# Strided attention: scores in two column halves, one turn of the weights, outputs over 64 rows

## The chip, the cores and the metric

The kernel runs on one core of a Trainium2 chip. The metric is the device time of one execution in microseconds. Three runs of the kernel before took 131.04, 131.12 and 131.29 us (median 131.12). One profiled execution of it took 130.88 us; its trace spans 129.0 us, and the remaining 1.8 us lie outside the first and the last instruction.

## The reference

```python
attend_positions = np.arange(0, seq, stride)          # 1024 / 64 = 16 keys per head
k = K[:, :, attend_positions, :]; v = V[:, :, attend_positions, :]
scores = einsum('bhqd,bhkd->bhqk', q, k) / sqrt(dim)  # every query, 16 keys
weights = exp(scores - max); weights /= sum + 1e-10
result = einsum('bhqk,bhkd->bhqd', weights, v)
```

Q, K, V and the result are (8, 12, 1024, 64) in fp32: 96 heads of 1024 queries with 64 elements. Q (25.2 MB) is read whole, of K and V every 64th row, and the result (25.2 MB) is written whole.

## The kernel before, in words

The 96 heads are worked in 24 groups of four (`NG`, index `g`). A group of Q is 1 MB; it lands in one of 16 buffers (`big[:, g % 16]`, 8 KB on each of 128 partitions), and the group's result is later written into the same buffer and stored from there. So the load of group g + 16 waits until the store of group g has landed.

For one group the engines do this:

- ACT (`cast_a`) and POOL (`cast_p`) cast the two halves of Q to bf16 (`qb`).
- DVE turns it in 32x32 blocks of bf16 pairs (`turn`, L362) into `qt`: the partitions then hold head (4) and pair of the 64 elements (32), the two elements of a pair lie side by side, and the columns are the tokens.
- PE makes the scores (`score_products`, L561). The stationary operand `k_cur` holds two heads' 16 keys in 32 columns. Two passes `f` (one for each element of a pair) add up; within a pass four matmuls of 32 columns and 512 tokens go to the four quarters of the array's columns (`tile_position`). The moving operand's innermost step is one pair, 4 bytes, 32 times.
- DVE turns the scores back from PSUM so that tokens lie on partitions (`lay`, L389) and takes the maximum over 16 keys (`highest`, L396).
- POOL subtracts it (L403), ACT takes the exponent (L409), DVE adds up (`sums`, L414) and inverts (`inverse`, L421), POOL multiplies and casts to bf16 (`normalise`, L428).
- DVE turns the weights (`back`, L438) in two operations of 64 partitions each. They fill the two diagonal blocks of `w_t`, a 128x128 matrix for each of 8 token sets; the other two blocks were set to zero once, at the start (L291).
- PE multiplies `w_t` with the values (`output_products`, L573): for each half `h` four matmuls over all 128 rows, 256 columns each. `v_cur` holds the four heads' values, each masked to its own rows.
- ACT copies the outputs from PSUM into the buffer (`evict`, L455), twice for a group.

Nothing is scheduled by a tool: the order is written out by hand. In the steady state DVE runs a loop of 20 groups (`dve_stream`, four rounds in its body) with the order `lay(g)`, `turn(g+1)`, `highest(g)`, `sums(g-1)`, `back(g-2)`, `inverse(g-1)`. PE runs a loop of its own: `score_products(g+3)`, then `output_products(g, 0)` and `(g, 1)`. Engines wait for each other through counting semaphores (`gates`). ACT and POOL run straight programs whose order follows the loop over `n`.

All transfers are issued by SP on one queue, in the order: the loads of 16 groups with the rows of K and V among the first, two stores, then store g and load g + 14 in turn for g = 2 to 9, then stores of two groups at once, the last of them (groups 22 and 23) after everything else. A store (`send`, L251) writes from each partition runs of 16 tokens, 4 KB.

Of the kernel before, what the change touches and what calls it, by code (L numbers as in the profile page):

```python
# [11 lines left out]
BF16 = mybir.dt.bfloat16  # L12
I16 = mybir.dt.int16
I32 = mybir.dt.int32
# [160 lines left out]
def kernel(  # L175
# [8 lines left out]
    nc = tc.nc  # L184
# [22 lines left out]
    k_all = sb.tile([P, NG, 2, 2, 32], BF16, name="k_all")  # L207
    identity = sb.tile([P, P], BF16, name="identity")
    perm_v = sb.tile([P, 2, 2, 2, 2, NK], BF16, name="perm_v")
# [12 lines left out]
    k_cur = sb.tile([P, 2, 2, 2, 32], BF16, name="k_cur")  # L222
    s_sel = sb.tile([P, 4], FP32, name="s_sel")

    spare, later = big[:, NB - 1], big[:, NB - 2]
# [47 lines left out]
    def constants():  # L273
        op("POOL", lambda: nc.gpsimd.memset(identity, 0.0), writes=["identity"])
        op("POOL", lambda: nc.gpsimd.affine_select(
            out=identity, in_=identity, compare_op=ALU.not_equal, fill=1.0, base=0,
            pattern=[[-1, P]], channel_multiplier=1,
        ), reads=["identity"], writes=["identity"])
        for c in range(2):
            for b in range(2):  # L280
                op("POOL", lambda c=c, b=b: nc.gpsimd.tensor_copy(
                    out=perm_v[:, c, b],
                    in_=_ap_with(
                        identity, [identity.ap[0], [0, 2], [32, 2], [1, NK]], 64 * c + 16 * b
                    ),
                ), reads=["identity"], writes=[f"perm{c}{b}"])
# [5 lines left out]
        op("DVE", lambda: nc.vector.tensor_reduce(  # L292
            out=s_sel,
            in_=identity.rearrange("p (b e u k) -> p u e b k", b=2, e=2, u=2),
            op=ALU.max, axis=mybir.AxisListType.XY,
        ), reads=["identity"], writes=["s_sel"])

# [7 lines left out]

    def keys(c, s, e):
        fn = nc.vector.tensor_copy if e == "DVE" else nc.scalar.copy
        src, b, u = 32 * (2 * c + s // 2), s % 2, s // 2
        op(e, lambda: fn(  # L309
            k_all[32 * s : 32 * s + 32, c::2, :, b, NK * u : NK * u + NK],  # L310
            k_r[src : src + 32].rearrange("p n (a k f) -> p a n f k", a=2, f=2)[:, b],
        ), reads=["k_r", "k_zero"], writes=[f"k{c}{s}"])

    def value_sums(n):
        for c in range(2):
            r = nc.tensor.matmul(  # L316
                o_ps[n][:, c, 0 : NC * D // 2],
                lhsT=perm_v[:, n].rearrange("p b e u k -> p (b e u k)"),
                rhs=v_bf[:, 6 * c : 6 * c + 6], start=True, stop=True,
            )  # L320
        return r

    def value_rows():
        op("POOL", lambda: nc.gpsimd.tensor_copy(out=v_bf, in_=v_raw), reads=["v_raw"],  # L324
           writes=["v_bf"], gate="stV")
        for n in range(2):
            op("PE", None, reads=["v_bf"] + [f"perm{n}{b}" for b in range(2)],
               writes=[f"o{n}"], gates=[("stV", 1)])

    def value_copy(n):  # L330
# [37 lines left out]
    def place_k(g):  # L368
        n = 1 if g < 2 else 2
        op("POOL", lambda: nc.gpsimd.tensor_copy(  # L370
            out=k_cur[:, g % 2 : g % 2 + n].rearrange("p g f b x -> p (g f b x)").bitcast(I32),
            in_=k_all[:, g : g + n].rearrange("p g f b x -> p (g f b x)").bitcast(I32),
        ), reads=["k_zero"] + [f"k{i % 2}{s}" for i in range(g, g + n) for s in range(4)],
           writes=[f"k_cur{i % 2}" for i in range(g, g + n)], gate=None if g == 1 else "stK")

# [50 lines left out]

    def normalise(g):
        op("POOL", lambda: nc.gpsimd.tensor_tensor(  # L428
            out=_ap_with(w_n[g % 2], [w_n[g % 2].ap[0], [64, 8], [1, 2], [32, 2], [2, NK]]),
            in0=ex[g % 2][:, :, 0:NK].rearrange("p (t x u) k -> p t x u k", x=2, u=2),  # L430
            in1=rec[g % 2].rearrange("p (t x u) -> p t x u", x=2, u=2).unsqueeze(4).to_broadcast([P, 8, 2, 2, NK]),
            op=ALU.mult,
        ), reads=[f"ex{g % 2}", f"rec{g % 2}"], writes=[f"w_n{g % 2}"], gate="wn")

    def back(g):
        for b in range(2):
            rows = slice(64 * b, 64 * b + 64)
            r = nc.vector.transpose(  # L438
                w_t[g % 2][rows, :, rows].bitcast(I32),
                w_n[g % 2][rows].rearrange("p n k -> p (n k)").bitcast(I32),  # L440
            )
        return r

    def weights_back(g, **how):
        op("DVE", lambda: back(g), reads=[f"w_n{g % 2}"], writes=[f"w_t{g % 2}"], gate="wt",
# [4 lines left out]
           gates=[("ev", 2 * g + h + 1)] + [("wt", g + 1)] * (h == 0) + [("stV", g // 2 + 2)] * (h == g % 2 == 0))  # L450

    def evict(g, h):
        o = o_ps[h].rearrange("p c (t x d) -> p x (c t) d", t=2, d=D)
        to = big[:, g % NB].rearrange("p (x t d) -> p x t d", x=4, t=8)[:, :, 4 * h : 4 * h + 4]
        op("ACT", lambda: nc.scalar.copy(to, o), reads=[f"o{h}"], writes=[f"b{g % NB}{'ab'[h]}"],  # L455
           gate=None if g == NG - 1 or (g, h) == (NG - 3, 1) else "ev")

# [95 lines left out]
    def pe_stream(sems, gates):  # L553
        pe = nc.tensor

        def score_products(g):
            for f in range(2):
                for e in range(2):
                    for b in range(2):
                        c = 2 * b + e  # L560
                        r = pe.matmul(  # L561
                            sc_ps[g % 2][32 * c : 32 * c + 32], lhsT=k_cur[:, g % 2, f, b],
                            rhs=_ap_with(
                                qt[g % 2], [qt[g % 2].ap[0], [D, 8], [16 * D, 2], [2, 32]],
                                extra_offset=8 * D * e + f,
                            ),
                            start=f == 0, stop=f == 1, tile_position=(0, 32 * c),
                        )
            r.then_inc(gates["sc"], 1)

        def output_products(g, h):
            for t in range(4):
                r = pe.matmul(  # L573
                    o_ps[h][:, t // 2, 256 * (t % 2) : 256 * (t % 2) + 256],
                    lhsT=w_t[g % 2][:, 4 * h + t],
                    rhs=v_cur[:, g % 2].rearrange("p x d -> p (x d)"),
                    start=True, stop=True,
                )
            r.then_inc(sems["PE"], 1)

        pe.wait_ge(gates["stV"], 1)
        for n in range(2):
            value_sums(n).then_inc(sems["PE"], 1)
        for g in range(AHEAD):
            pe.wait_ge(gates["turned"], g + 1)
            if g % 2 == 0:
                pe.wait_ge(gates["stK"], g // 2 + 1)
            score_products(g)
        with pe.Fori(0, NG // TURN):
            for j in range(TURN):  # L590
                pe.wait_ge(gates["turned"], j + AHEAD + 1)
                if j:
                    pe.wait_ge(gates["stK"], (j + AHEAD) // 2 + 1)
                score_products(j + AHEAD)
                for h in range(2):
                    pe.wait_ge(gates["ev"], 2 * j + h + 1)
                    if h == 0:
                        pe.wait_ge(gates["wt"], j + 1)
                        if j == 0:
                            pe.wait_ge(gates["stV"], 2)  # L600
                    output_products(j, h)
            for name, n in (("turned", TURN), ("wt", TURN), ("ev", 2 * TURN), ("stK", 1), ("stV", 1)):
                pe.sem_inc(gates[name], -n)
# [64 lines left out]
```

## Time and profile before

| what | before |
|---|---|
| median of three runs | 131.12 us |
| the profiled execution, its span | 130.88 us, 129.0 us |
| busy: DVE, ACT, POOL, PE | 107.5, 90.3, 84.2, 66.9 us |
| bytes moved, mean rate over the span | 51.15 MB, 396 GB/s |
| DMA queue of SP: share of 16 engines' time | 94.7% |
| one 64x256 turn of the weights (48 of them) | 435 ns |
| two score passes of one group on PE | 1.04 us |
| eight output matmuls of one group on PE | 1.87 us |

An engine's busy time counts overlapping instructions once. The chain of waits follows the work that ended last back from the end. The table of stages gives for any stretch the busy time of each engine, the granted clock of PE, the share of the 16 DMA engines' time that packets took, and the rate.

### The profile page before, as it was taken

To read this page: it belongs to the slowest core of one execution; us is meant where nothing else is said; L and a number is where in the kernel's file an instruction comes from. 1 tells how busy PE (TensorE), PEld (TensorE's weight loads), DVE (VectorE), ACT (ScalarE), POOL (GpSimd) and SP (SyncE) were. 2 spreads that over 40 slices of the span, in tenths; PEclk is the share of its full clock that TensorE was granted. 3 is DMA by queue.
4 is the path that set the end of the run, shared out by engine and by line. 5 is a ranking of instruction groups with operands and counts; after the bars stand their busy time and mean duration, and the time that the engine had idled before them with its cause. 6 is when DMAs were issued, how large, how long until landed. Compare 5 with 4: busy or idle time off the path is not lost.

```text
span 129.0 us, 1514 instructions
## 1 busy us (share of the span) xinstructions
PE 66.9 (52%) x412; PEld 26.4 (20%) x412; DVE 107.5 (83%) x185; ACT 90.3 (70%) x106; POOL 84.2 (65%) x110
## 2 busy tenths in 40 slices
PE   0000620338766654667865478666486668498000
PEld 0000100003332122312332123321133213234000
DVE  4739699499999999999999999999999999982000
ACT  3034877747788998798879888789877876778400
POOL 4016650949777987779877797777977777643000
PEclk9999999999999999555558655557855555959955
DMA  3999999999999899998998998998999996396993
GB/s 71 341 385 470 427 396 467 437 396 457 416 427 447 361 429 424 434 485 366 437 477 366 455 470 361 460 480 361 432 442 411 416 432 269 163 472 259 452 442 163
DMA packets 6803, 51.15 MB, mean 396 GB/s; under 512 B 3760, under 2 KB 3760, under 8 KB 3760
## 3 DMA queue, kind: packets, MB, share of 16 engines
q1 hardware_dynamic: 6800, 51.12, 94.7%
q14 instruction: 3, 0.02, 0.1%
HBM read 25.95 MB, written 25.17 MB: 396 GB/s over the span
## 4 chain that ended last, share of the span: by engine, by line
DVE 70%; DMA 6%; PE 4%; issue 4%; POOL 3%; ACT 2%; SPq 2%; DVEq 1%; ACTq 1%; POOLq 0%
DVE qt L362 20%; DVE s_t L389 11%; DVE w_t L438 11%; DVE top L396 11%; DVE total L414 11%; DMA big<-in_V_dram 6%; DVE rec L421 6%; PE o L573 2%; DVE v_all L340 2%; PE sc L561 1%; SPq L34 1%; POOL w_n L428 1%; POOL s_t L403 1%; ACT big L455 1%; ACT qb L353 1%
## 5 line engine op out<-in xcount | busy, mean ns | idle before, releaser
L455 ACT COPY big<-o 128x1024 f32<-128x1024 f32 x48 | 46.3, 1016 | 14.1 <-PE o L573 14.1
L573 PE MATMUL o<-v_cur,w_t 128*128 128x256 bf16 x192 | 39.1, 371 | 22.8 <-DVE w_t L438 20.8
L428 POOL TENSOR_TENSOR w_n<-ex,rec 128x512 bf16<-128x512 f32 x24 | 25.5, 1061 | 15.9 <-DVE rec L421 15.9
L561 PE MATMUL sc<-qt,k_cur 128*32 128x512 bf16 x216 | 26.6, 584 | 17.1 <-DVE qt L362 10.6
L573 PEld LDWEIGHTS o<-v_cur,w_t 128*128 128x128 bf16 x192 | 22.3, 125 | 49.6 <-issue 39.8
L403 POOL TENSOR_TENSOR s_t<-s_t,top 128x512 f32<-128x512 f32 x24 | 25.4, 1058 | 7.1 <-DVE top L396 7.1
L362 DVE STREAM_TRANSPOSE qt<-qb 128x1024 int32<-128x1024 int32 x24 | 28.8, 1200 | 0.0
L353 ACT CAST qb<-big 128x1024 bf16<-128x1024 f32 x24 | 25.2, 1055 | 0.0
L358 POOL CAST qb<-big 128x1024 bf16<-128x1024 f32 x24 | 25.0, 1044 | 0.1
L438 DVE STREAM_TRANSPOSE w_t<-w_n 64x256 int32<-64x256 int32 x48 | 20.9, 435 | 1.9 <-POOL w_n L428 1.6
L409 ACT ACTIVATE ex<-s_t 128x512 f32<-128x512 f32 x24 | 15.3, 638 | 6.8 <-POOL s_t L403 6.8
L389 DVE STREAM_TRANSPOSE s_t<-sc 128x512 f32<-128x512 f32 x24 | 15.8, 660 | 1.6 <-PE sc L561 1.6
L414 DVE TENSOR_REDUCE total<-ex 128x32 f32<-128x544 f32 x24 | 16.9, 706 | 0.0
L396 DVE TENSOR_REDUCE top<-s_t 128x32 f32<-128x512 f32 x24 | 15.5, 647 | 0.1
L561 PEld LDWEIGHTS sc<-qt,k_cur 128*32 128x32 bf16 x216 | 3.7, 104 | 30.2 <-DVE qt L362 22.8
L421 DVE RECIPROCAL rec<-total 128x32 f32<-128x32 f32 x24 | 8.5, 353 | 0.7
L316 PE MATMUL o<-big,perm_v 128*128 128x384 bf16 x4 | 1.5, 521 | 12.7 <-POOL big L324 12.7
L378 POOL COPY v_cur<-v_all 128x256 int32<-128x256 int32 (+1 forms) x13 | 5.0, 384 | 1.1 <-PE o L573 1.1
L370 POOL COPY k_cur<-k_all 128x128 int32<-128x128 int32 (+1 forms) x13 | 3.7, 281 | 2.1 <-ACT k_all L309 1.8
L299 ACT CAST big<-big 128x384 bf16<-128x384 f32 x1 | 0.5, 512 | 5.4 <-DMA big<-in_K_dram 5.4
L300 POOL CAST big<-big 128x384 bf16<-128x384 f32 x1 | 0.5, 507 | 5.3 <-DMA big<-in_K_dram 5.3
L309 DVE COPY k_all<-big 32x384 bf16<-32x384 bf16 x6 | 3.5, 588 | 0.1
(19 smaller groups left out, 16.8 us busy)
## 6 DMA issues: line engine op xcount, KB each, us to landing
big<-in_Q_dram SPq DMA_DIRECT2D x24, 1024.0 KB, 12.2
out_dram<-big SPq DMA_DIRECT2D x7, 2048.0 KB, 7.7
out_dram<-big SPq DMA_DIRECT2D x10, 1024.0 KB, 14.1
big<-in_K_dram SPq DMA_DIRECT2D x1, 384.0 KB, 6.5
big<-in_V_dram SPq DMA_DIRECT2D x1, 384.0 KB, 7.9
```

What stands on the lines that cost most here:

```text
L353: op("ACT", lambda: nc.scalar.copy(b[:, half:], q[:, half:]), reads=[f"b{g % NB}{h}" for h in "ab"], writes=[f"qb{g % 4}1"])
L358: op("POOL", lambda: nc.gpsimd.tensor_copy(out=b[:, 0:half], in_=q[:, 0:half]), reads=[f"b{g % NB}{h}" for h in "ab"] + [f"qb{g % 4}1"] * ...
L362: return nc.vector.transpose(qt[g % 2].bitcast(I32), qb[g % 4].bitcast(I32))
L389: return nc.vector.transpose(s_t[g % 2].rearrange("p n k -> p (n k)"), sc_ps[g % 2])
L396: return nc.vector.tensor_reduce(out=top[g % 2], in_=s_t[g % 2], op=ALU.max, axis=mybir.AxisListType.X)
L403: op("POOL", lambda: nc.gpsimd.tensor_tensor(out=s_t[g % 2], in0=s_t[g % 2], in1=top[g % 2].unsqueeze(2).to_broadcast([P, 32, NK]), op=ALU ...
L414: return nc.vector.tensor_reduce(out=total[g % 2], in_=ex[g % 2], op=ALU.add, axis=mybir.AxisListType.X)
L428: op("POOL", lambda: nc.gpsimd.tensor_tensor(out=_ap_with(w_n[g % 2], [w_n[g % 2].ap[0], [64, 8], [1, 2], [32, 2], [2, NK]]), in0=ex[g % 2 ...
L438: r = nc.vector.transpose(w_t[g % 2][rows, :, rows].bitcast(I32), w_n[g % 2][rows].rearrange("p n k -> p (n k)").bitcast(I32),)
L455: op("ACT", lambda: nc.scalar.copy(to, o), reads=[f"o{h}"], writes=[f"b{g % NB}{'ab'[h]}"], gate=None if g == NG - 1 or (g, h) == (NG - 3, ...
L561: r = pe.matmul(sc_ps[g % 2][32 * c : 32 * c + 32], lhsT=k_cur[:, g % 2, f, b], rhs=_ap_with(qt[g % 2], [qt[g % 2].ap[0], [D, 8], [16 * D, ...
L573: r = pe.matmul(o_ps[h][:, t // 2, 256 * (t % 2) : 256 * (t % 2) + 256], lhsT=w_t[g % 2][:, 4 * h + t], rhs=v_cur[:, g % 2].rearrange("p x ...
```

## The change

Scores: the stationary operand now holds the keys of all four heads in 64 columns (`k_cur` keeps its size), and a pass consists of two matmuls for the two halves of the array's columns, where there were four for the quarters. The two halves take alternating tokens. The moving operand is still 512 columns, but its dimensions are in another order: the innermost one is now a jump of 16 tokens (2 KB), twice, and the 4-byte step lies outside of it.

Weights: `back` is one operation over 128 partitions, and `w_t` has half the columns and no zero blocks; the two fills at the start are gone. `normalise` writes in the new order.

Outputs: each matmul contracts 64 rows (four heads times 16 keys) of one token half `e`; the halves sit in the upper and the lower 64 rows of the array (`tile_position`) and write to different PSUM banks. There are still four matmuls of 256 columns per half `h`.

Result and stores: `evict` copies the same amount in another order, and a partition now holds 8 consecutive tokens of each of four heads where it held 16 tokens of each of two. So a store writes runs of 2 KB, twice as many. The selection matrices for the values (`perm_v`) are made by two copies instead of four, and `keys` writes to other columns.

DVE's loop body, one round of four, before:

```order
L389 STREAM_TRANSPOSE s_t_73<-sc_90 128x512
L362 STREAM_TRANSPOSE qt_72<-qb_70 128x1024
L396 TENSOR_REDUCE top_81<-s_t_73 128x32
L414 TENSOR_REDUCE total_84<-ex_76 128x32
L438 STREAM_TRANSPOSE w_t_79<-w_n_77 64x8x32 x2
L421 RECIPROCAL rec_86<-total_84 128x32
```

and with the change:

```order
L384 STREAM_TRANSPOSE s_t_73<-sc_90 128x512
L357 STREAM_TRANSPOSE qt_72<-qb_70 128x1024
L391 TENSOR_REDUCE top_81<-s_t_73 128x32
L409 TENSOR_REDUCE total_84<-ex_76 128x32
L431 STREAM_TRANSPOSE w_t_79<-w_n_77 128x256
L416 RECIPROCAL rec_86<-total_84 128x32
```

The round keeps its order; the two turns of the weights are one. On SP's queue, behind the last of the first loads, the stores before:

```order
L34 DMA big<-in_Q_dram 128x2048 x14
L34 DMA out_dram<-big 128x2x1024 x3
L34 DMA big<-in_Q_dram 128x2048
L34 DMA out_dram<-big 128x2x1024
L34 DMA big<-in_Q_dram 128x2048
```

and with the change:

```order
L34 DMA big<-in_Q_dram 128x2048 x14
L34 DMA out_dram<-big 128x4x512 x3
L34 DMA big<-in_Q_dram 128x2048
L34 DMA out_dram<-big 128x4x512
L34 DMA big<-in_Q_dram 128x2048
```

The order of transfers is the same; each store goes from two runs of 1024 elements per partition to four of 512.

The core of the diff:

```diff
-    w_t = [sb.tile([P, 8, P], BF16, name=f"w_t{i}") for i in range(2)]
+    w_t = [sb.tile([P, 4, P], BF16, name=f"w_t{i}") for i in range(2)]
...
-            _ap_with(out, [[16 * D, P], [2 * SD, 2 * n], [1, 16 * D]], g * HG * SD),
+            _ap_with(out, [[8 * D, P], [SD, HG * n], [1, 8 * D]], g * HG * SD),
...
-        for i in range(2):
-            op("DVE", lambda i=i: nc.vector.memset(w_t[i], 0.0), writes=[f"w_t{i}"])
...
-        src, b, u = 32 * (2 * c + s // 2), s % 2, s // 2
+        src = 32 * (2 * c + s // 2)
         op(e, lambda: fn(
-            k_all[32 * s : 32 * s + 32, c::2, :, b, NK * u : NK * u + NK],
-            k_r[src : src + 32].rearrange("p n (a k f) -> p a n f k", a=2, f=2)[:, b],
+            k_all[32 * s : 32 * s + 32, c::2, :, NK * s : NK * s + NK],
+            k_r[src : src + 32].rearrange("p n (a k f) -> p a n f k", a=2, f=2)[:, s % 2],
...
-            out=_ap_with(w_n[g % 2], [w_n[g % 2].ap[0], [64, 8], [1, 2], [32, 2], [2, NK]]),
+            out=_ap_with(w_n[g % 2], [w_n[g % 2].ap[0], [1, 2], [64, 8], [32, 2], [2, NK]]),
...
     def back(g):
-        for b in range(2):
-            rows = slice(64 * b, 64 * b + 64)
-            r = nc.vector.transpose(
-                w_t[g % 2][rows, :, rows].bitcast(I32),
-                w_n[g % 2][rows].rearrange("p n k -> p (n k)").bitcast(I32),
-            )
-        return r
+        return nc.vector.transpose(
+            w_t[g % 2].rearrange("p t m -> p (t m)").bitcast(I32),
+            w_n[g % 2].rearrange("p n k -> p (n k)").bitcast(I32),
+        )
...
-        o = o_ps[h].rearrange("p c (t x d) -> p x (c t) d", t=2, d=D)
-        to = big[:, g % NB].rearrange("p (x t d) -> p x t d", x=4, t=8)[:, :, 4 * h : 4 * h + 4]
+        o = o_ps[h].rearrange("p e (t s d) -> p s t e d", t=2, d=D)
+        to = big[:, g % NB].rearrange("p (s t e d) -> p s t e d", s=4, t=4, e=2)[:, :, 2 * h : 2 * h + 2]
...
                 for e in range(2):
-                    for b in range(2):
-                        c = 2 * b + e
-                        r = pe.matmul(
-                            sc_ps[g % 2][32 * c : 32 * c + 32], lhsT=k_cur[:, g % 2, f, b],
-                            rhs=_ap_with(
-                                qt[g % 2], [qt[g % 2].ap[0], [D, 8], [16 * D, 2], [2, 32]],
-                                extra_offset=8 * D * e + f,
-                            ),
-                            start=f == 0, stop=f == 1, tile_position=(0, 32 * c),
-                        )
+                    r = pe.matmul(
+                        sc_ps[g % 2][64 * e : 64 * e + 64], lhsT=k_cur[:, g % 2, f],
+                        rhs=_ap_with(
+                            qt[g % 2], [qt[g % 2].ap[0], [2 * D, 8], [2, 32], [16 * D, 2]],
+                            extra_offset=D * e + f,
+                        ),
+                        start=f == 0, stop=f == 1, tile_position=(0, 64 * e),
+                    )
...
-            for t in range(4):
-                r = pe.matmul(
-                    o_ps[h][:, t // 2, 256 * (t % 2) : 256 * (t % 2) + 256],
-                    lhsT=w_t[g % 2][:, 4 * h + t],
-                    rhs=v_cur[:, g % 2].rearrange("p x d -> p (x d)"),
-                    start=True, stop=True,
-                )
+            for t in range(2):
+                for e in range(2):
+                    rows = slice(64 * e, 64 * e + 64)
+                    r = pe.matmul(
+                        o_ps[h][:, e, 256 * t : 256 * t + 256], lhsT=w_t[g % 2][rows, 2 * h + t],
+                        rhs=v_cur[rows, g % 2].rearrange("p s d -> p (s d)"),
+                        start=True, stop=True, tile_position=(64 * e, 0),
+                    )
```

More of the change, by code (lines that the diff above doesn't have):

```diff
@@ L206 @@
     edge = sb.tile([P, 32], FP32, name="edge")
-    k_all = sb.tile([P, NG, 2, 2, 32], BF16, name="k_all")
+    k_all = sb.tile([P, NG, 2, 4 * NK], BF16, name="k_all")
     identity = sb.tile([P, P], BF16, name="identity")
-    perm_v = sb.tile([P, 2, 2, 2, 2, NK], BF16, name="perm_v")
+    perm_v = sb.tile([P, 2, 2, 4 * NK], BF16, name="perm_v")
     v_cur = sb.tile([P, 2, 4, D], BF16, name="v_cur")
@@ L221 @@
     v_all = sb.tile([P, NG, 4, D], BF16, name="v_all")
-    k_cur = sb.tile([P, 2, 2, 2, 32], BF16, name="k_cur")
+    k_cur = sb.tile([P, 2, 2, 4 * NK], BF16, name="k_cur")
     s_sel = sb.tile([P, 4], FP32, name="s_sel")
@@ L279, in constants @@
         for c in range(2):
-            for b in range(2):
[L281 to L284, printed above, removed]
-                    ),
-                ), reads=["identity"], writes=[f"perm{c}{b}"])
+            op("POOL", lambda c=c: nc.gpsimd.tensor_copy(
+                out=perm_v[:, c],
+                in_=_ap_with(identity, [identity.ap[0], [0, 2], [1, 4 * NK]], 64 * c),
+            ), reads=["identity"], writes=[f"perm{c}"])
         op("DVE", lambda: nc.vector.memset(k_all, 0.0), writes=["k_zero"])
@@ L289, in constants @@
             op("DVE", lambda i=i: nc.vector.memset(ex[i], EPS), writes=[f"ex{i}"])
-        for i in range(2):
-            op("DVE", lambda i=i: nc.vector.memset(w_t[i], 0.0), writes=[f"w_t{i}"])
         op("DVE", lambda: nc.vector.tensor_reduce(
             out=s_sel,
-            in_=identity.rearrange("p (b e u k) -> p u e b k", b=2, e=2, u=2),
+            in_=identity.rearrange("p (e s k) -> p s e k", e=2, s=4),
             op=ALU.max, axis=mybir.AxisListType.XY,
@@ L317, in value_sums @@
                 o_ps[n][:, c, 0 : NC * D // 2],
-                lhsT=perm_v[:, n].rearrange("p b e u k -> p (b e u k)"),
+                lhsT=perm_v[:, n].rearrange("p e k -> p (e k)"),
                 rhs=v_bf[:, 6 * c : 6 * c + 6], start=True, stop=True,
@@ L326, in value_rows @@
         for n in range(2):
-            op("PE", None, reads=["v_bf"] + [f"perm{n}{b}" for b in range(2)],
+            op("PE", None, reads=["v_bf", f"perm{n}"],
                writes=[f"o{n}"], gates=[("stV", 1)])
@@ L370, in place_k @@
         op("POOL", lambda: nc.gpsimd.tensor_copy(
-            out=k_cur[:, g % 2 : g % 2 + n].rearrange("p g f b x -> p (g f b x)").bitcast(I32),
-            in_=k_all[:, g : g + n].rearrange("p g f b x -> p (g f b x)").bitcast(I32),
+            out=k_cur[:, g % 2 : g % 2 + n].rearrange("p g f x -> p (g f x)").bitcast(I32),
+            in_=k_all[:, g : g + n].rearrange("p g f x -> p (g f x)").bitcast(I32),
         ), reads=["k_zero"] + [f"k{i % 2}{s}" for i in range(g, g + n) for s in range(4)],
@@ L428, in normalise @@
         op("POOL", lambda: nc.gpsimd.tensor_tensor(
-            out=_ap_with(w_n[g % 2], [w_n[g % 2].ap[0], [64, 8], [1, 2], [32, 2], [2, NK]]),
-            in0=ex[g % 2][:, :, 0:NK].rearrange("p (t x u) k -> p t x u k", x=2, u=2),
-            in1=rec[g % 2].rearrange("p (t x u) -> p t x u", x=2, u=2).unsqueeze(4).to_broadcast([P, 8, 2, 2, NK]),
+            out=_ap_with(w_n[g % 2], [w_n[g % 2].ap[0], [1, 2], [64, 8], [32, 2], [2, NK]]),
+            in0=ex[g % 2][:, :, 0:NK].rearrange("p (x t u) k -> p x t u k", x=2, u=2),
+            in1=rec[g % 2].rearrange("p (x t u) -> p x t u", x=2, u=2).unsqueeze(4).to_broadcast([P, 2, 8, 2, NK]),
             op=ALU.mult,
```

2 lines of the change are left out of this document (removed).

## The prediction

> **What bounds the kernel now.** I read the page first: its slices, its queue and the head of its chain.
>
> ```profile
> DVE  4739699499999999999999999999999999982000
> DMA  3999999999999899998998998998999996396993
> q1 hardware_dynamic: 6800, 51.12, 94.7%
> DVE 70%; DMA 6%; PE 4%; issue 4%; POOL 3%; ACT 2%; SPq 2%; DVEq 1%; ACTq 1%; POOLq 0%
> ```
>
> Two things are full at once. DVE is at nine tenths or more from slice 9 to 35 and is 70% of the chain, and the DMA engines are as full, except in slices 34, 35 and 37 near the end. So I read the chain for one group, and then the stages for DMA.
>
> ```profile
> 59.93 0.63 DVE total L414
> 60.56 0.34 DVE w_t L438
> 60.90 0.01 issue
> 60.92 0.44 DVE w_t L438
> 61.36 0.03 issue
> 61.39 0.35 DVE rec L421
> 61.74 0.57 DVE s_t L389
> 62.31 1.12 DVE qt L362
> 63.43 0.57 DVE top L396
> 64.00 0.63 DVE total L414
> ```
>
> One round is 64.00 - 59.93 = 4.07 us of DVE without a gap. Nothing else ends a wait in it: DVE sets the pace of the computation. The stages (after the span in us, each engine's busy us; the last three numbers are PE's clock, the DMA share and GB/s):
>
> ```profile
> 52.00:84.00 32.00, 21.63 (x128) 8.98 (x128) 31.64 (x56) 26.45 (x32) 26.33 (x31) 0.55 1.01 428
> 20.00:40.00 20.00, 10.69 (x64) 3.79 (x64) 18.24 (x31) 14.34 (x19) 14.11 (x19) 1.00 1.00 428
> 90.00:107.00 17.00, 11.21 (x68) 4.86 (x69) 16.82 (x31) 13.17 (x16) 13.88 (x17) 0.57 1.00 425
> 2.00:14.00 12.00, 1.34 (x4) 0.44 (x4) 8.75 (x14) 3.66 (x6) 4.47 (x10) 1.00 1.04 373
> 106.00:122.00 16.00, 10.30 (x72) 4.62 (x72) 10.32 (x21) 11.38 (x13) 7.16 (x8) 0.79 0.76 324
> 109.00:111.00 2.00, 1.01 (x11) 0.69 (x8) 1.96 (x5) 0.95 (x3) 1.25 (x2) 0.89 0.00 0
> ```
>
> Only loads run at 20 to 40 us, loads and stores in turn at 52 to 84, only stores at 90 to 107: the share is 1.00 to 1.01 and the rate 425 to 428 GB/s in all three, so about 428 is all that the engines give. A round reads and writes 2 x 1.05 MB in 4.07 us, which would need 515. The stores therefore pile up behind the computation, and it is the transfers that run late until about 108 us. Only then has the queue caught up: nothing moves from 109 to 111 us, and over 106 to 122 the share is 0.76, so 16 x 0.24 = 3.84 us are idle. **Those 3.84 us are all that a faster computation can win**; the rest of the span is transfer.
>
> **The change, part by part.** The turn of the weights, first. Groups of instructions (shape, busy us, mean ns):
>
> ```profile
> L438 DVE STREAM_TRANSPOSE w_t<-w_n 64x256 int32<-64x256 int32 x48 | 20.9, 435 | 1.9 <-POOL w_n L428 1.6
> L362 DVE STREAM_TRANSPOSE qt<-qb 128x1024 int32<-128x1024 int32 x24 | 28.8, 1200 | 0.0
> L302 DVE STREAM_TRANSPOSE big<-big 128x384 int32<-128x384 int32 x1 | 0.6, 578 | 2.8 <-POOL big L300 2.8
> ```
>
> The two rows with 128 partitions give (1200 - 578) / (1024 - 384) = 0.97 ns a column and 205 ns fixed, so 454 ns at 256 columns; the row with 64 partitions has 435. Partitions cost nothing, columns do. In the chain the pair takes 61.39 - 60.56 = 0.83 us, one operation 0.44 + 0.03 = 0.47: **0.36 us less in a round**. The bounds are 0.34 (by 454 ns) and 0 (if 128 partitions cost two halves, against which the three rows speak). A round becomes 3.71 us, and 24 turns give up to 8.6 us.
>
> Do the others follow? Between 52 and 84 us, 32 / 4.07 = 7.9 rounds, ACT is busy 26.45 / 7.9 = 3.36 us a round and POOL 3.35, both under 3.71. So DVE keeps the pace, and where it waited for nobody it has 0.36 us less until each wait; the scores are the one that could come late.
>
> ```profile
> 63.49 1.04 PE L561 MATMUL sc<-qt,k_cur 128*32 128x512 bf16 x8 [0.16 <-DVE qt L362]
> 65.73 0.65 DVE L389 STREAM_TRANSPOSE s_t<-sc 128x512 f32<-128x512 f32 x1
> 61.46 1.87 PE L573 MATMUL o<-v_cur,w_t 128*128 128x256 bf16 x8 [0.99 <-DVE w_t L438]
> ```
>
> The scores end at 64.53 and DVE reads them at 65.73: 1.20 us of cover, 0.84 after the change. Eight matmuls become four, in two passes of two side by side where there were two of four. Two passes of 512 columns at the rate of the outputs (1.87 us for 2048 columns, at most 0.91 ns each) would be 0.93 us, and 1.04 is what stands: a pass runs its matmuls side by side, and the number beside each other does not count. So 1.04 us if the new order of the stream costs nothing. No row shows a stream that jumps 2 KB at every element; the nearest is L309, DVE copies with a 4-byte step, against L340, an operation on unbroken rows:
>
> ```profile
> L309 DVE COPY k_all<-big 32x384 bf16<-32x384 bf16 x6 | 3.5, 588 | 0.1
> L340 DVE TENSOR_SCALAR v_all<-big,s_sel 128x768 bf16<-128x768 bf16 x4 | 2.3, 626 | 1.2 <-ACT qb L353 1.2
> ```
>
> 1.53 against 0.82 ns an element is a factor of 1.9, 1.98 us for the scores; below 1.04 nothing speaks. Cover ends at 1.04 + 0.84 = 1.88, so even the upper bound costs only 0.10 us a round. I take zero, since the present 4-byte step costs this engine nothing. [...]
>
> The outputs: if the two 64-row halves run side by side, 1.87 us falls towards 1.0; if one after the other, it stays. ACT's copies follow sooner or as now, and after the change the end hangs on transfers, so I cost this at nothing. Without that cover it would be worth at most 0.9 us once, at the end. The copies and the multiplication on POOL keep their size and their innermost runs: nothing, and 0.25 us of slack in a round on each engine (3.71 - 3.36 and more) if they grow. The two fills and the shorter copies at the start lie before the keys arrive (DVE waits 2.8 us there, row L302): nothing.
>
> **The stores.** They go from 256 to 512 runs a MB; 24 groups make 6144 more. From the stages: 1.05 MB takes 2450 ns at 428 (loads, 128 pieces of 8 KB on the partitions' side) and 2467 at 425 (stores, 256 runs of 4 KB): 17 x 16 / 128 = 2.1 ns of one engine for a run. That is 6144 x 2.1 / 16 = **0.8 us** of transfer. Upper bound, the 3072 rows of 256 B of K and V between 2 and 14 us: 373 x 12 = 4476 KB would take 10.46 us at 428, the share is 1.04 x 12 = 12.48, so 2.02 x 16 / 3072 = 10.5 ns a row, and 4.0 us for the change. Lower bound 0. I take 0.8: 2 KB is nearer to 4 KB than to 256 B. [...]
>
> **Is everything early enough** for transfers without a gap? The last copies of groups 19, 21 and 23, one late load's issue and its first use:
>
> ```profile
> 107.29 1.93 ACT L455 COPY big<-o 128x1024 f32<-128x1024 f32 x2 [0.82 <-PE o L573]
> 114.46 1.93 ACT L455 COPY big<-o 128x1024 f32<-128x1024 f32 x2 [0.82 <-PE o L573]
> 118.94 1.93 ACT L455 COPY big<-o 128x1024 f32<-128x1024 f32 x2 [0.17 <-PE o L573]
> 77.75 0.53 SPq L34 DMA_DIRECT2D big<-in_Q_dram  x1
> big<-in_Q_dram SPq DMA_DIRECT2D x24, 1024.0 KB, 12.2
> 100.97 1.05 ACT L353 CAST qb<-big 128x1024 bf16<-128x1024 f32 x1
> ```
>
> The queue runs dry at about 109 us; from there three stores of 2.1 MB take 4.9 us each. So the next must be issued by about 107, 112 and 117 us. The copies end at 109.2, 116.4 and 120.9 now, and 20, 22 and 24 turns at 0.36 us bring them to 102.0, 108.5 and 112.2. A third of the gain is spare; 0.19 us a round would do. The last load, issued at 77.75 and some 12.2 us under way, lands at 90; its cast moves from 101.0 to about 94. The computation still doesn't wait for loads.
>
> **Sum**, against the profiled execution: 130.88 - 3.84 + 0.8 = 127.8 us. The median shown lies 0.24 above that execution, so 128.1 against it; I say **128.0 us**, 2.4% faster. DVE's 8.6 us turn into 3.
>
> **Rivals.**
>
> *The stores cost more.* At the price of the 256 B rows 4.0 us are lost and 3.84 won: 131.0 against the execution, no change. For: nothing in this trace writes 2 KB runs. Against: the step from 8 to 4 KB is hardly visible. In between, at 4 to 9 ns a run, it would be 128.6 to 130.5.
>
> *The scores become the bound, and it gets slower.* Place: `score_products`, whose stream jumps 2 KB at every element. Below 1.88 us it is hidden; at 1.04 + 1.20 = 2.24 us a round is back at 4.07 and all is lost, and from there it decides. A stream at a third of today's rate takes 3 x 1.04 = 3.12 us, 0.88 more than that in 20 rounds: 130.9 + 17.6 = 148.5 us. For: no stream of PE in this trace does that. [...] Against: the factor of 1.9 in the nearest rows, at which a round would be 3.81 us and transfers still the bound.
>
> *The turn does not get cheaper*, since 128 partitions cost what two halves of 64 do: a round stays at 4.07 us, the last store is issued when it is now and takes some 0.1 us more (two twenty-fourths of 0.8): 131.0, no change. Against: the three rows of L438, L362 and L302.
>
> **How the numbers follow.** The forecast, 127.2 to 128.6, gets 0.62; stores between (128.6 to 130.6) 0.14; stores at the price of the rows (around 131) 0.06; scores 0.09; the turn 0.04; anything else slower 0.05, among it stores that fall below 400 GB/s, at which 25.2 MB take 3.7 us more than at 425 and the win is gone. The range 126.9 to 130.6 reaches from transfers without a gap and without a price (127.0) to the end of the second case and leaves out about 2 in 10. A measurement of this kernel tells 0.2% from nothing. Faster: 0.62 + 0.14 and a little of the scores' case, 0.78. The same: 0.08. Slower: 0.14.
>
> **What would show it.** Right: the turn of the weights one row of 24 at 435 to 454 ns; a round of 3.7 us in the chain; DMA at nine tenths in all slices up to the last, with no empty stretch after 105 us; the chain ending in a long wait for stores after ACT's last copy at about 112 us; 420 GB/s or more in a stretch of stores alone. Wrong: a wait of DVE at `lay` for PE (scores over 1.9 us), a stretch of stores near 400 GB/s or below at a full share, a turn near 0.87 us, or idle DMA that stays, for which I would have no reason.

## The result and the profile after

The changed kernel takes 128.89 us (median of six runs, 128.61 to 129.03) against 131.09 us for the kernel before (six runs, 131.04 to 131.29). The ratio is 0.9826 with a 95% interval of 0.9813 to 0.9839: 1.7% faster, where 2.4% (128.0 us) was forecast. The profiled execution took 128.61 us, with a span of 126.5 us.

The page of the changed kernel, with the slices of DVE and DMA, SP's queue and the head of its chain:

```profile
DVE  4329699499999999999999999999999981000000
DMA  3899999999999989989989989999999999999992
q1 hardware_dynamic: 6800, 51.12, 97.4%
DVE 64%; PE 6%; DMA 5%; ACT 3%; POOL 3%; issue 3%; ACTq 1%; DVEq 1%; SPq 0%
```

DVE is done in slice 34, and the last slices are transfer alone. The hole that DMA had in slices 34, 35 and 37 is gone. One round of DVE in the chain (start us, us, what):

```profile
59.72 0.62 DVE total L409
60.35 0.35 DVE w_t L431
60.70 0.23 DVE rec L416
60.93 0.57 DVE s_t L384
61.51 1.12 DVE qt L357
62.63 0.57 DVE top L391
63.20 0.63 DVE total L409
```

It takes 3.48 us, shorter than the 3.71 forecast: beside the second turn, the remaining one takes 0.12 us less in the chain (0.35, where 0.44 + 0.03 stood) and the inverse 0.12 less (0.23 against 0.35), since the inverse now begins before the turn has ended (at 60.62, the turn ends at 60.70). The groups of the turn and of the two products of PE:

```profile
L551 PE MATMUL sc<-qt,k_cur 128*64 128x512 bf16 x108 | 34.6, 720 | 28.5 <-DVE qt L357 23.3
L565 PE MATMUL o<-v_cur,w_t 64*128 64x256 bf16 x192 | 24.7, 402 | 7.0 <-DVE w_t L431 5.1
L431 DVE STREAM_TRANSPOSE w_t<-w_n 128x256 int32<-128x256 int32 x24 | 10.4, 434 | 1.4 <-POOL w_n L423 1.4
```

A turn of 128 partitions costs 434 ns, what one of 64 did (435). The scores' matmuls became longer (720 ns in the mean, 584 before).

The stage that answers to the one with idle DMA before (clock, DMA share and GB/s at the end), and the last microseconds of the changed kernel and then of the kernel before. The view counts a packet whole in the stretch in which it starts, so that a short stretch can read over 1:

```profile
106.00:122.00 16.00, 2.57 (x18) 0.54 (x16) 0.37 (x1) 3.85 (x4) 0.00 (x0) 0.64 1.00 420
...
123.00:123.50 0.50, 0.00 (x0) 0.00 (x0) 0.00 (x0) 0.00 (x0) 0.00 (x0) 0.50 1.02 426
123.50:124.00 0.50, 0.00 (x0) 0.00 (x0) 0.00 (x0) 0.00 (x0) 0.00 (x0) 0.50 0.86 360
124.00:124.50 0.50, 0.00 (x0) 0.00 (x0) 0.00 (x0) 0.00 (x0) 0.00 (x0) 0.50 0.47 197
124.50:125.00 0.50, 0.00 (x0) 0.00 (x0) 0.00 (x0) 0.00 (x0) 0.00 (x0) 0.50 0.16 66
```

```profile
126.50:127.00 0.50, 0.00 (x0) 0.00 (x0) 0.00 (x0) 0.00 (x0) 0.00 (x0) 0.50 1.22 524
127.00:127.50 0.50, 0.00 (x0) 0.00 (x0) 0.00 (x0) 0.00 (x0) 0.00 (x0) 0.50 0.02 0
```

The share from 106 to 122 us went from 0.76 to 1.00: the 3.84 us are filled. But the end is another: before, DMA stopped from full to nothing within half a microsecond; now it runs out over 1.5 us, and 0.14, 0.53 and 0.84 of three half microseconds, 0.76 us, are lost there. The forecast has no term for that, and the execution lies 128.61 - 127.84 = 0.77 us above it. That the two agree so closely is in part chance: other small terms, taken apart further down, nearly cancel.

### The profile page after: what moved, and what is told of

It is laid out like the page before. It is cut to its first block, busy times and chain, and to the rows that moved or that the text cites. A ratio compares the mean times of both kernels' runs of the same rounds, so it can differ in the third digit from the quotient of the medians.

```text
span 126.5 us, 1270 instructions
## 1 busy us (share of the span) xinstructions
PE 60.4 (48%) x304; PEld 17.1 (14%) x304; DVE 93.9 (74%) x159; ACT 90.4 (71%) x106; POOL 84.1 (66%) x108
## 4 chain that ended last, share of the span: by engine, by line
DVE 64%; PE 6%; DMA 5%; ACT 3%; POOL 3%; issue 3%; ACTq 1%; DVEq 1%; SPq 0%
DVE qt L357 20%; DVE s_t L384 12%; DVE top L391 11%; DVE total L409 11%; DMA big<-in_K_dram 5%; DVE w_t L431 5%; PE sc L551 4%; DVE rec L416 3%; PE o L565 2%; DVE v_all L335 2%; POOL qb L353 1%; POOL s_t L398 1%; ACT k_all L304 1%; ACT big L447 1%; ACT qb L348 1%
## 5 line engine op out<-in xcount | busy, mean ns | idle before, releaser
L551 PE MATMUL sc<-qt,k_cur 128*64 128x512 bf16 x108 | 34.6, 720 | 28.5 <-DVE qt L357 23.3
L565 PE MATMUL o<-v_cur,w_t 64*128 64x256 bf16 x192 | 24.7, 402 | 7.0 <-DVE w_t L431 5.1
L565 PEld LDWEIGHTS o<-v_cur,w_t 64*128 64x128 bf16 x192 | 11.6, 123 | 34.8 <-ACT big L447 23.4
L431 DVE STREAM_TRANSPOSE w_t<-w_n 128x256 int32<-128x256 int32 x24 | 10.4, 434 | 1.4 <-POOL w_n L423 1.4
L551 PEld LDWEIGHTS sc<-qt,k_cur 128*64 128x64 bf16 x108 | 5.0, 140 | 43.3 <-DVE qt L357 35.8
L416 DVE RECIPROCAL rec<-total 128x32 f32<-128x32 f32 x24 | 7.5, 311 | 0.0
L297 DVE STREAM_TRANSPOSE big<-big 128x384 int32<-128x384 int32 x1 | 0.6, 579 | 4.2 <-POOL big L295 4.2
```

Source lines behind the costliest of these rows:

```text
L431: return nc.vector.transpose(w_t[g % 2].rearrange("p t m -> p (t m)").bitcast(I32), w_n[g % 2].rearrange("p n k -> p (n k)").bitcast(I32),)
L551: r = pe.matmul(sc_ps[g % 2][64 * e : 64 * e + 64], lhsT=k_cur[:, g % 2, f], rhs=_ap_with(qt[g % 2], [qt[g % 2].ap[0], [2 * D, 8], [2, 32] ...
L565: r = pe.matmul(o_ps[h][:, e, 256 * t : 256 * t + 256], lhsT=w_t[g % 2][rows, 2 * h + t], rhs=v_cur[rows, g % 2].rearrange("p s d -> p (s ...
```

## The experiments

Each ratio is to runs of the kernel before beside it on the same chip. Chips differ a little (the kernel before had 131.09 us beside the result, and 130.93, 130.86 and 130.66 on the three of the experiments): kernels whose stores and transfers were those of the changed kernel came out at 0.9826, 0.9858 and 0.9865, so differences under 0.4% between experiments on different chips are not read.

**Is the end set by DVE or by transfers? A fill in DVE's round.**

```diff
+    pad = sb.tile([P, 240], FP32, name="pad")
...
                 inverse(g - 1).then_inc(sems["DVE"], 1)
+                dve.memset(pad, 0.0)
```

> The changed kernel with a fill of a spare tile (128 x 240 fp32, about 0.28 us) at the end of each of DVE's 20 rounds. Theory (transfers end it, DVE has about 0.4 us a round to spare): a round of 3.75 us, the same median, 128.9 us. Rival (DVE's round still sets the end): 20 x 0.28 = 5.6 us more, 134.5 us.

Measured: 129.16 us, ratio 0.9858 (0.9841 to 0.9876). One round of DVE's timeline, from turn to turn and cut to three lines, and the stage near the end:

```profile
59.60 1.19 DVE L358 STREAM_TRANSPOSE qt<-qb 128x1024 int32<-128x1024 int32 x1
62.58 0.26 DVE L614 MEMSET pad<- 128x240 f32 x1
63.34 1.19 DVE L358 STREAM_TRANSPOSE qt<-qb 128x1024 int32<-128x1024 int32 x1
...
106.00:122.00 16.00, 5.96 (x36) 1.28 (x36) 2.09 (x6) 6.68 (x8) 2.75 (x4) 0.80 1.01 421
```

The round went to 3.74 us, 0.26 more in each of 20, 5.2 us of DVE. The ratio is that of the two other kernels below with the changed kernel's transfers (0.9858 and 0.9865), and DMA stayed full. So DVE's round does not set the end any more, and 0.26 us of the gain in each round were not needed.

**Does the gain come from the turn? Two turns of 64 partitions in the changed kernel.**

```diff
-        return nc.vector.transpose(
-            w_t[g % 2].rearrange("p t m -> p (t m)").bitcast(I32),
-            w_n[g % 2].rearrange("p n k -> p (n k)").bitcast(I32),
-        )
+        for b in range(2):
+            rows = slice(64 * b, 64 * b + 64)
+            r = nc.vector.transpose(
+                w_t[g % 2][rows].rearrange("p t m -> p (t m)").bitcast(I32),
+                w_n[g % 2][rows].rearrange("p n k -> p (n k)").bitcast(I32),
+            )
+        return r
```

> The changed kernel with the turn of the weights in two operations of 64 partitions again; all else is the changed kernel. Theory (the whole gain comes from DVE's round): the second turn costs 0.35 us, and the inverse behind it starts only after it has ended, another 0.24 us, so a round goes from 3.47 to about 4.06 us as before the change, DMA falls idle again near the end and the median is 131.1 to 131.4 us. If the inverse still starts before the turn has ended: a round of 3.82 us, still inside the slack, 128.9 to 129.3 us. Rival (the gain came from the shorter outputs or the new layout): 128.9 us at a round of 4.06 us.

Measured: 131.84 us, ratio 1.0075 (1.0061 to 1.0088). Chain and stage:

```profile
60.67 0.34 DVE w_t L433
61.02 0.01 issue
61.03 0.44 DVE w_t L433
61.47 0.03 issue
61.51 0.35 DVE rec L416
...
106.00:122.00 16.00, 9.34 (x56) 2.69 (x56) 10.44 (x21) 11.48 (x13) 7.09 (x8) 1.00 0.83 331
```

The round is 4.07 us again, DMA is idle again near the end, and the kernel is slower than the one before. The whole gain hangs on this one operation; the shorter outputs and the new layout bring nothing that shows by themselves, since the kernel before with nothing but the 2 KB runs of the stores, below, comes out at nearly the same ratio (1.0069). That it ends above 131.4 was not expected; that experiment tells why.

**Why does the second turn cost 0.59 us and not 0.36?** Two ways to split the turn in another manner. First the same two operations in reverse order (`for b in (1, 0)`):

> The changed kernel with the turn of the weights in two operations of 64 partitions, partitions 64 to 127 first, then 0 to 63. If the inverse could not start early because the operation ahead of it begins at partition 64: it starts early again, a round of about 3.82 us, 128.9 to 129.3 us. If it is because the operation ahead covers half of the partitions that the inverse works on: it stays late, a round of 4.06 us, 131.1 to 131.4 us.

Measured: 131.28 us, ratio 1.0037 (1.0023 to 1.0052). The chain:

```profile
60.44 0.03 issue
60.47 0.44 DVE w_t L433
60.91 0.01 issue
60.93 0.44 DVE w_t L433
61.36 0.23 DVE rec L416
```

Both answers fell: the inverse starts early again (0.23 us), as the first had it, and yet the round is 4.05 us, as the second had it. The lost overlap only moved. Now it is the first turn, on partitions 64 to 127, that waits for the operation ahead to end, and the second that waits for the first. So the halves were cut by columns instead, both over all partitions (the loop over the two halves, `b`, is left out):

```diff
-            w_t[g % 2].rearrange("p t m -> p (t m)").bitcast(I32),
-            w_n[g % 2].rearrange("p n k -> p (n k)").bitcast(I32),
+            w_t[g % 2][:, 2 * b : 2 * b + 2].rearrange("p t m -> p (t m)").bitcast(I32),
+            w_n[g % 2][:, 16 * b : 16 * b + 16].rearrange("p n k -> p (n k)").bitcast(I32),
...
```

> The changed kernel with the turn of the weights in two operations over all 128 partitions, each for half of the columns. Theory (what costs 0.24 us more than the second turn itself is that an operation which starts at partition 64 does not overlap with its neighbours): the two overlap like any others, about 0.2 us for the first (0.435 less 0.97 ns for 128 columns, less the overlap) and 0.35 together with the inverse's early start, a round of at most 3.65 us, and the median stays at 128.9 us. Rival (any second operation costs that much): a round of 4.0 us and 131.2 us or more.

Measured: 128.88 us, ratio 0.9865 (0.9838 to 0.9892). The chain:

```profile
60.54 0.41 DVE w_t L432 x2
60.95 0.23 DVE rec L416
```

Two operations over all partitions take 0.41 us together, 0.06 more than one, and the inverse starts early. It is not the number of operations that cost 0.59 us, but that one of them works on partitions 64 to 127. In the kernel before and in both orders of the two turns that one begins 0.01 to 0.03 us after the operation ahead has ended, and what follows it begins 0.01 to 0.03 us after its end; this holds beside the turn on 0 to 63 too. Everywhere else in these rounds an operation begins 0.06 to 0.09 us before the one ahead of it ends.

**What does a run of a store cost?** Stores of 4 KB and of 1 KB runs in the changed kernel.

```diff
-            _ap_with(out, [[8 * D, P], [SD, HG * n], [1, 8 * D]], g * HG * SD),
+            _ap_with(out, [[16 * D, P], [2 * SD, 2 * n], [1, 16 * D]], g * HG * SD),
```

For 1 KB the new line reads `[[4 * D, P], [SD // 2, 2 * HG * n], [1, 4 * D]]`.

> The changed kernel with the stores' pattern of the kernel before: runs of 4 KB, 6144 fewer of them. The rows land in other places of the result than they should; everything else is the changed kernel. Theory (transfers end it, a store run costs about 2.6 ns of one engine, from the 16 KB packets that went from 616 to 626 ns): DMA time falls by 6144 x 2.6 / 16 = 1.0 us, the median from 128.9 to 127.9 us, and a stretch of stores alone goes from 419 back to 425 GB/s. Rival (shorter runs cost nothing, the 0.9 us missing to the forecast went elsewhere): 128.9 us. Rival (the computation ends it): 128.9 us, and idle DMA appears near the end.

> The changed kernel with stores in runs of 1 KB, 12288 more than in the changed kernel; the rows land in other places of the result. Theory (a fixed price of about 2.6 ns a run): 12288 x 2.6 / 16 = 2.0 us more, 130.9 us, stores alone at about 408 GB/s. Rival (the price grows with shorter runs towards that of the 256-byte rows, 10.5 ns): up to 8 us more, 137 us. Rival (runs cost nothing): 128.9 us.

Measured: 127.87 us with 4 KB (ratio 0.9775, 0.9759 to 0.9791) and 130.23 us with 1 KB (0.9947, 0.9934 to 0.996). The stage from 106 to 122 us, where stores alone run, first with 4 KB and then with 1 KB (the changed kernel: 1.00 and 420):

```profile
106.00:122.00 16.00, 2.42 (x16) 0.44 (x14) 0.23 (x1) 3.85 (x4) 0.00 (x0) 0.63 1.01 427
```

```profile
106.00:122.00 16.00, 2.15 (x16) 0.37 (x12) 0.18 (x1) 3.73 (x4) 0.00 (x0) 0.67 1.01 410
```

On one chip, 18432 runs more cost 130.23 - 127.87 = 2.36 us: 2.36 x 16 / 18432 = 2.0 ns of an engine for a run. In the records of the packets (16 KB in 4, 8 or 16 runs) the mean goes from 616 to 626 and 645 ns: 2.5 and 2.3 ns a run. The price is about fixed and does not climb towards the 10.5 ns that the prediction worked out for the 256-byte rows. For this change it is 0.8 to 1.0 us.

**The same runs in the kernel before**, where DMA has idle time to take them in: the changed store pattern alone.

> The kernel before with the changed stores alone: runs of 2 KB, twice as many; the rows land in other places of the result. Theory (before, the computation sets when the last store starts, so the price of the runs falls into idle DMA time, except in the last store): about 0.1 us more, 131.2 us, idle DMA near the end shrinks from 3.8 to about 2.9 us. Rival (the price of the runs always counts): 1.0 us more, 132.1 us.

Measured: 131.73 us, ratio 1.0069 (1.0057 to 1.0081), 0.87 us slower. Here the theory missed. The stage near the end, of this kernel:

```profile
106.00:122.00 16.00, 10.54 (x72) 4.72 (x72) 10.05 (x20) 10.96 (x13) 7.15 (x8) 0.71 0.86 343
112.00:117.00 5.00, 4.26 (x36) 1.92 (x40) 3.29 (x9) 4.01 (x6) 3.18 (x4) 0.78 0.95 367
92.00:104.00 12.00, 6.47 (x52) 2.82 (x48) 11.87 (x22) 10.56 (x13) 9.92 (x14) 0.78 1.01 423
```

The idle time did shrink (the share rises from 0.76 to 0.86), and the last store's first packet starts at 122.6 us, as before the edit (122.5). But in both kernels that is the moment at which the store ahead of it ends on the first of the engines: the computation sets when the store before the last one starts (117.5 us here, 117.6 before the edit), and the last one follows without a gap. So the runs of two stores count, and not of one.

More than that, the two stores that start behind a gap run worse than those ahead of it: 367 GB/s at a share of 0.95, against 423 at 1.01. Their packets take 670 ns in the mean where 626 is usual, single ones up to 927; the last store, which follows without a gap, has 627 again. With 4 KB runs the same two stores had 614 and 617. From its first packet to the mean of its engines' ends (how they are found is told below) the store before the last takes 5.40 us where it took 4.97; the last one adds 4.98 where it added 4.87, and its slowest engine ends 0.36 us behind the mean where it was 0.08. Less the 0.13 us by which the first of the two starts earlier, this is 0.69 us, of 0.72 between the two profiled executions (131.60 and 130.88). The run above with two turns has the same (672 and 666 ns), which is why it too lies above the kernel before.

**Do the engines fall out of step?** The last store waits until the one before it has landed.

```diff
             nc.sync.wait_ge(sems["ACT"], counts["ACT"])
+            nc.sync.wait_ge(sems["out4"], counts["out4"])
```

> The changed kernel with one wait more: SP issues the last store (groups 22 and 23) only when the store before it has landed, so that all 16 DMA engines stand empty and start it together. Theory (in the changed kernel the engines reach the end at different times, because no gap lets the late ones catch up): the last store costs some 2 us of waiting and starting, about 131 us in all, but its end is steeper: the DMA share falls from full to nothing in well under half of the 1.5 us that it takes in the changed kernel. Rival (the ramp at the end belongs to the last store with 2 KB runs itself): a ramp of about 1.5 us again.

Measured: 132.21 us, ratio 1.0105 (1.008 to 1.013). The end of the store before the gap, and of the one behind it:

```profile
118.00:119.00 1.00, 0.00 (x0) 0.00 (x0) 0.00 (x0) 0.00 (x0) 0.00 (x0) 0.50 0.98 410
119.00:119.50 0.50, 0.00 (x0) 0.00 (x0) 0.00 (x0) 0.00 (x0) 0.00 (x0) 0.50 0.55 229
119.50:120.00 0.50, 0.00 (x0) 0.00 (x0) 0.00 (x0) 0.00 (x0) 0.00 (x0) 0.50 0.32 131
120.00:120.50 0.50, 0.00 (x0) 0.00 (x0) 0.00 (x0) 0.00 (x0) 0.00 (x0) 0.50 0.08 33
...
123.50:127.50 4.00, 0.00 (x0) 0.00 (x0) 0.00 (x0) 0.00 (x0) 0.00 (x0) 0.50 0.99 377
127.50:128.00 0.50, 0.00 (x0) 0.00 (x0) 0.00 (x0) 0.00 (x0) 0.00 (x0) 0.50 1.10 459
128.00:128.50 0.50, 0.00 (x0) 0.00 (x0) 0.00 (x0) 0.00 (x0) 0.00 (x0) 0.50 0.48 197
128.50:129.00 0.50, 0.00 (x0) 0.00 (x0) 0.00 (x0) 0.00 (x0) 0.00 (x0) 0.50 0.01 0
```

The store that came without a gap runs out over 1.5 us again (0.45, 0.68 and 0.92 of three halves lost); of the one that the engines began together almost no packet starts after 128.5. The time is 1.2 us above the 131 expected. The wait is longer than 2 us: from 120.91, where the slowest engine ends, to 123.15, and 3.3 us in the mean of the engines. And this store too was slow from its common start: 377 GB/s at a full share, packets of 668 ns in the mean and up to 931, which makes it 0.4 us longer.

The packet records show the step as well. They do not name the engine, but they hold 16 packets of 4 bytes for each of the 43 transfers, and from 60 us on all but a few of them start within 4 ns of the end of a data packet. They are read here as the end of the transfer on each of 16 engines:

```
a transfer ends on its 16 engines, us                     first     last     mean
kernel before, the first load                              5.09     6.27     5.51
kernel before, the store ahead of the gap                108.15   109.26   108.78
kernel before, the store behind the gap                  116.65   116.80   116.72
kernel before, the last store                            127.38   127.53   127.45
changed kernel, the first load                             4.75     6.28     5.30
changed kernel, the fourth store from the end            108.92   110.39   109.65
changed kernel, the last store                           123.87   125.34   124.60
last store waits, the store ahead of the gap             119.08   120.91   119.81
last store waits, the last store                         128.14   128.89   128.53
```

In the kernel before, too, the engines are out of step, by 1.1 us, until its gap; behind it they end within 0.15 us of each other. The changed kernel has no gap and keeps 1.47 us to its end. With the wait, 1.82 us become 0.75. That is half of the changed kernel's 1.47 and not well under half, as was expected, so a part of the ramp stays with the 2 KB runs behind a gap; the kernel before with 2 KB runs ends over 0.75 us as well. How far apart the engines are at the end differs between executions: 1.41 us with the old order of the scores, 2.13 with the fill in DVE's round, with the same stores. In all twelve kernels they are 0.7 to 1.5 us apart at the end of the first load already. In the eight with 2 KB runs the distance grows by 0.4 to 0.8 us at the third store (from 1.09 to 1.47 in the changed kernel), in the three with 4 KB runs by at most 0.02 there; so shorter runs have a share in it.

**The scores' stream.** The old order of dimensions in the changed kernel, and the new order in the kernel before:

```diff
-                            qt[g % 2], [qt[g % 2].ap[0], [2 * D, 8], [2, 32], [16 * D, 2]],
+                            qt[g % 2], [qt[g % 2].ap[0], [2 * D, 8], [16 * D, 2], [2, 32]],
```

> The changed kernel with the scores' moving operand in the old order of dimensions (4-byte step innermost, 32 times). Scores come out in another order of tokens, so the result's rows are permuted. Theory (the jump of 2 KB at every element is what slowed the stream): the second pass starts about 427 ns after the first instead of 577, the scores of a group take 1.04 us instead of 1.28; it is hidden, so the median stays at 128.9 us. Rival (two matmuls of 64 columns side by side are slower than four of 32, whatever the order): 1.28 us stays.

> The kernel before with the scores' moving operand in the new order (a jump of 2 KB innermost, twice), four matmuls of 32 columns side by side as before; the result's rows are permuted. Theory (the order sets the stream's pace): the scores of a group go from 1.04 to about 1.28 us while PE's clock is low, and stay well above 0.64 us where it is high; hidden behind 1.20 us of cover, so the time stays at 131.1 us. Rival (the order does not matter): 1.04 us, and 0.64 us at the high clock.

Measured: 128.88 us with the old order in the changed kernel (ratio 0.9858, 0.9843 to 0.9872), and 130.91 us with the new order in the kernel before (one run; 130.86 beside it). The scores of one group: in the changed kernel, in the changed kernel with the old order, in the kernel before with the new one, with its stage:

```profile
62.68 1.28 PE L551 MATMUL sc<-qt,k_cur 128*64 128x512 bf16 x4 [0.80 <-DVE qt L357]
```

```profile
62.07 1.06 PE L551 MATMUL sc<-qt,k_cur 128*64 128x512 bf16 x4 [0.80 <-DVE qt L357]
```

```profile
63.53 1.28 PE L561 MATMUL sc<-qt,k_cur 128*32 128x512 bf16 x8 [0.99 <-DVE qt L362]
...
52.00:84.00 32.00, 19.55 (x132) 7.19 (x128) 31.64 (x56) 27.73 (x33) 26.37 (x32) 0.89 1.01 428
```

The order alone makes the stream slower, 1.28 against 1.06 us, whatever the number of matmuls side by side. Neither time moved: it is hidden. In the third kernel the granted clock is mostly full (0.89 between 52 and 84 us), and all 27 groups still take 1.28 to 1.34 us (1.29 at 59.5 us, where the record has the clock at a half, and 1.28 at 63.5, where it is full), so this stream's pace does not follow the clock. The kernel before has a group of 0.64 us at the full clock: there the new order would be half as fast.

## Why the prediction was right, and where it was off

- **What can be won is idle DMA, not DVE's time**: right. DVE is 13.6 us less busy (93.9 against 107.5 us), the time fell by 2.2 us, and a round lengthened by 0.26 us changed nothing. The prediction calls a third of the gain spare; its own 0.19 of 0.36 us leave nearly half.
- **The turn, 0.36 us a round**: too small. One operation costs what was forecast (434 ns), but 0.59 us fell away, because the turn on partitions 64 to 127 had kept its neighbours from overlapping. The step that failed is the 0.44 + 0.03 taken from the chain for the remaining operation; it carried the second turn's lost overlap with it. Nothing hung on it, since the gain was beyond what transfers allow.
- **Copies and loads early enough**: right; the last copy ends at 109.2 us, where 112.2 was forecast, and the share is 1.00 from 106 to 122 us.
- **The outputs, cost nothing**: right. The two halves run side by side, eight matmuls of a group in 1.04 us instead of 1.87, and with the two turns put back nothing of it shows in the time.
- **The scores at 1.04 us, cost zero**: the size was wrong, 1.28 us, inside the bounds given (1.04 to 1.98), and the cost was zero, by the cover that the prediction had counted and not by the reason that it gave for 1.04. Of the 1.20 us of cover 0.37 are left (the scores end at 63.96, DVE reads at 64.33). The new order took 1.28 us where the old one took 1.06 in the same kernel at the low clock, 1.2 times as long. Why the order does this, no run shows.
- **The stores, 0.8 us**: 0.8 to 1.0 us. The choice of the 4 KB row as the nearest held down to 1 KB. The 2.1 ns a run that it took from there were measured as 2.0 to 2.5.
- **The sum, 130.88 - 3.84 + 0.8**: here the forecast lost its 0.8 us. It took the idle time as the mean of 16 engines, and the time ends with the last of them. The mean of the engines' ends moved from 127.45 to 124.60, by 2.85 us (3.84 less 1.0 for the runs would be 2.84); but the last one lay 0.08 us behind the mean before and lies 0.74 us behind it now. The gap had let the late engines catch up, and filling it took that away. With the 0.09 us that the execution needs less behind its last packet this makes 2.85 - 0.66 + 0.09 = 2.28 us, and 130.88 - 128.61 = 2.27 was measured. These are measured ends, so their sum has to close; what tests the account is the 2.85 against 2.84. The lateness of the last engine is no fixed price: with the same stores it was 0.66 us in the run with the old order of the scores and 1.21 in the one with the fill. That a gap brings the engines back in step is shown by the kernel before itself and by the run with the wait. What puts them out of step is open: they are so from the first load on, in both kernels.
- **The rivals**: stores at the price of 256-byte rows, scores as the bound and a turn that gets no cheaper are each excluded by a run or a row above.

## What to carry to other kernels

Where a computing engine and the transfers are both full, ask for how long the transfers would still be idle if the engine were free: that is the win, and not the engine's saved time. Take the idle time from the engine that finishes last, since a gap in which all wait for the next transfer also put them back in step here: 1.12 us apart ahead of it, 0.15 behind it. In the kernel before that engine stands idle from 109.26 to 111.77 us and from 116.80 to 117.61, 3.32 us and not 3.84; 130.88 - 3.32 + 0.8 would have given 128.4 us, where 128.61 was measured. The turn on half of the partitions took as long here as one on all of them (435 and 434 ns), and the one in the upper half cost its neighbours their overlap.

## What the runs showed of the hardware

- A DVE turn on partitions 64 to 127 overlapped neither with the operation ahead of it nor with the one behind it, in either order of the two halves; the same work over all partitions in two operations cost 0.06 us more than in one, against 0.59 us.
- A moving operand of PE that jumps 2 KB at every element streamed two passes of 512 columns in 1.28 to 1.34 us at either clock; with a 4-byte step it took 1.04 to 1.06 us at the low clock and 0.64 at the full one.
- The 16 DMA engines ended the first load 0.7 to 1.5 us apart and stayed 0.7 us or more apart in a queue that never emptied, 1.1 to 2.1 us at its end; behind a gap they ended within 0.15 us of each other with 4 KB runs, and 0.7 to 0.8 us with 2 KB.
- Stores with 2 KB runs took 626 ns for a packet of 16 KB in a queue that never emptied (420 to 423 GB/s), and 666 to 672 ns in a store that started behind a gap, when all engines began together. With 4 KB runs the kernel before shows no such loss (617 ns, and 614 and 617 behind its gaps). Why is open.
- The column of the granted clock can't be read ahead of the first entry of its record. In the kernel before that entry is at 44.6 us; the column reads 1.00 from 20 to 40 us, but the scores take 1.05 us and the outputs 1.86 there, as they do later at 0.50, and 0.64 and 1.03 at a recorded 1.00 (47.2 and 45.2 us). In the changed kernel the first entry is at 107.2 us. The same holds for the run with the old order of the scores, whose 1.06 us up to there are the low clock's pace.
